# Token-major products of 512 columns, fed by two weight transfers of four row chunks

## The chip, the cores and the metric

The kernel runs on one core of a Trainium2 chip. The metric is the device time of one execution in microseconds (us). The profiler records the span of an execution, every instruction with its start and its length, and the clock that TensorE was granted.

## The reference, cut to what matters

The input is one sequence of 256 positions with 1024 features, and a memory of the same shape. Two blocks of two layers each follow one another. All is float32.

```python
# block 1, twice:
proj = h @ w_in[l]          # 1024 x 5376: xr, gr, q, k, v, g_rnn, g_attn
merged = sigmoid(g_rnn) * (y_rnn @ w_br_rnn) + sigmoid(g_attn) * (y_attn @ w_br_attn)
h = layer_norm(ALPHA * h + merged @ w_out)
h = layer_norm(ALPHA * h + cross_attention(h, mem) @ co_w)   # cq_w, ckv_w inside
h = layer_norm(ALPHA * h + (silu(gate) * up) @ ffn_wo)       # gate, up = h @ ffn_wi
# block 2, twice:
proj = rms_norm(x) @ w_in[l]     # q, k, v, z_a, u_h, z_h, g_a, g_h
merged = sigmoid(g_a) * (y_a @ w_pa) + sigmoid(g_h) * (y_h @ w_ph)
x = x + rms_norm(merged @ w_out)     # y_h: two long convolutions by Fourier transform
```

## The kernel before

Every weight matrix is streamed once. The sync engine's queue brings a chunk of 1 MB (`raw`, three buffers); a chunk is used in two halves of 128 x 1024 numbers. ScalarE rounds each half to a high part `wh` (line 229), VectorE subtracts for the low part `wl` (line 231), and both have four buffers. The activations are kept in such pairs too. One product is three matmuls, high times high, high activation times low weight, low activation times high weight (`mm3`).

There are two forms. `fm` (feature-major) holds the weights still in the array and moves 256 positions past them. `tm` (token-major, lines 406 to 446) holds a 128 x 128 piece of the activations still and moves weight columns past it. It makes the products whose results are wanted with one position per partition: q, k and v of `w_in`, the values of the cross attention (`ckv_w`), `w_out` and `co_w` in block 1, v and z_a of `w_in_2`, and `w_out_2` in block 2. The down projection of the feed-forward (`ff`) has a form of its own, with 512 columns in a matmul.

In `tm`, a group is 256 columns, one chunk of eight row chunks x 256 columns. The first half brings row chunks 0 to 3, the second 4 to 7. In each half the 12 matmuls of the first 128 positions (block 0) come ahead of the 12 of the second (block 1), so a group holds two PSUM tiles, each of which is read out (`evac`) after its last matmul. In the last group block 1's first half is kept back (`hold`), so that block 0 is done early. PSUM has eight banks, four of them in the pool `pa` (`pch`), which `tm` shares with the transposes (`tx`), the attention scores and the Fourier products (`dft`, `c`).

What follows a `tm` depends on the readout. `ln_evac` adds the residual (line 569), takes statistics (571, 574), and normalises (586); then `to_fm` transposes the result (`tx`), applies gain and bias (479 on ScalarE, 485 on VectorE, into `f`) and splits it (`h1h`, `h1l` after the first norm, `h2`, `h3` after the others, 350 and 351), four pairs of row chunks one after another. Then GpSimd multiplies and adds the gain and bias to the token-major copy (605, 606). In block 2 `evo` squares and sums on ScalarE (`jk`, 1679) and multiplies on VectorE (`xo`, 1680), and `evv` makes v and z_a (`za`).

TensorE's and the sync queue's order is written out as the program is generated: a clock `self.t` adds n / 2.4 ns for a matmul of n columns, and stages of the side chains (`pump`) are put in where their estimated times have come. The order on VectorE, ScalarE and GpSimd is set by the tile scheduler.

Of the kernel before, what the change touches and what calls it, by code (L numbers as in the profile page):

```python
# [13 lines left out]
F32 = mybir.dt.float32  # L14
# [6 lines left out]
P = 128  # L21
D = 1024
KD = D // P
S = 256
# [14 lines left out]
LATE = ((0, 0), (1, 0), (1, 1))  # filters whose products fill gaps of the tensor engine  # L39
# [5 lines left out]
# estimated time from the issue of a stage until its results are there, ns  # L45
# [10 lines left out]
def shape_constants():  # L56
# [9 lines left out]
    # odd frequencies of length 2 S: g = f + 1/2 for f < P; those of 2 P - g follow from the  # L66
    # sums over even and odd positions
# [22 lines left out]
class Chunk:  # L90
    """One weight transfer of [P, a, b], used in two halves (by column or by row)."""
# [12 lines left out]
class Net:  # L104
    def __init__(self, ctx, tc, a):
# [12 lines left out]
        # splits of weights wait while a norm holds the vector engine, then queue behind .defer  # L118
# [9 lines left out]
    # ------------------------------------------------------------------ order of issue  # L128
    # Chains are generators that issue a stage and yield the time until the next one can start;
    # the weight stream runs between their stages.  # L130
# [14 lines left out]
    def pump(self):  # L145
        """issues the stages that are due"""
        while True:
            due = [c for c in self.chains if c.ready <= self.t]
            if not due:
                return  # L150
            self.advance(due[0], self.chains)

    def idle(self, until=None):
        """tensor engine has nothing to do: background stage, or let time pass"""
        for c in self.bg:
            if c.ready <= self.t:
                self.advance(c, self.bg)
                return
        nxt = [c.ready for c in self.chains + self.bg if c.ready > self.t]
        if until is not None:  # L160
            nxt.append(until)
        self.t = max(self.t, min(nxt))
# [15 lines left out]
    def run_stream(self, gen):  # L178
        """items: Chunk, or a function to call when its turn comes"""
# [95 lines left out]
    def pin(self):  # L275
        """queues the block's work behind the latest split of weights"""
# [5 lines left out]
    # ------------------------------------------------------------------ tiles  # L282
# [10 lines left out]
    def fmt(self, name, n=2, dt=F32):  # L293
        """feature-major tensor, 4 chunks of [P, S] to a tile"""
# [27 lines left out]
    def tmp(self, shape, name="s", dt=F32):  # L322
        """short-lived: released by the stage that takes it"""
# [3 lines left out]
    def keep(self, shape, name="s", dt=F32):  # L327
        """lives over a few stages of a chain"""
# [19 lines left out]
    # ------------------------------------------------------------------ building blocks  # L348
# [26 lines left out]
    def fm(self, w, c0, ncols, x, evac, kc=KD):  # L375
        """chunks of x() @ w, feature-major; evac(pair, psum)"""
        step = 2048 // kc
        nm = step // 2 // P
        for c in range(c0, c0 + ncols, step):
            box = {}  # L380

            def half(h, wh, wl, c=c, box=box):
                xx = x()
                for i in range(h * nm, h * nm + nm):
# [4 lines left out]
                    # parts of one kind together: the others may still be on their way  # L389
# [16 lines left out]
    def tm(self, w, c0, ncols, x, evac):  # L406
        """chunks of x() @ w, token-major, 256 columns each; evac(chunk, block, psum)"""
        for c in range(c0, c0 + ncols, 256):
            box = {}
            last = c + 256 == c0 + ncols  # L410
            ci = (c - c0) // 256

            def part(h, tb, wt, ps):
                xx = x()
                t = slice(tb * P, tb * P + P)
                if self.start:
                    # the lo part of the weights comes last
                    for j in range(3):
                        for k in range(4):
# [4 lines left out]
                for k in range(4):  # L424
                    g = h * 4 + k
                    self.mm3(ps, self.ch2(xx, g, t), (wt[0][:, k, :], wt[1][:, k, :]),
                             g == 0, g == KD - 1)

            def first(wh, wl, box=box, last=last, part=part):
                box["ps"] = [self.pch([256], "tm") for _ in range(TB)]  # L430
                box["w"] = wh, wl
                part(0, 0, (wh, wl), box["ps"][0])
                if not last:
                    self.pump()
                    part(0, 1, (wh, wl), box["ps"][1])

            def second(wh, wl, box=box, last=last, part=part, ci=ci):
                part(1, 0, (wh, wl), box["ps"][0])
                evac(ci, 0, box["ps"][0])
                self.pump()  # L440
                if last:
                    part(0, 1, box["w"], box["ps"][1])
                part(1, 1, (wh, wl), box["ps"][1])
                evac(ci, 1, box["ps"][1])
            yield Chunk([(None, w[:, c:c + 256].rearrange("(k p) f -> p k f", p=P))], KD, 256,
                        False, [first, second], hold=last)
# [9 lines left out]
    def to_fm(self, src, x, scale=None):  # L456
        """chain: token-major [P, D] per block -> split feature-major x; gain and bias"""
# [31 lines left out]
    def load_x(self, src, name, n=1):  # L489
        """token-major loads, in n column parts"""  # L490
# [7 lines left out]
    # ------------------------------------------------------------------ block 1  # L498
# [58 lines left out]
    def ln_evac(self, t, h, n=256, f=1.0, gb=None, pause=False):  # L557
        """evac for tm: t = f * ALPHA * h + psum, psum being f times the branch, and its
        statistics; normalises a full block, with gain and bias if given"""
# [38 lines left out]
    def ln_co(self, l, i, t, hT):  # L598
        """chain: normalised t -> hT (split feature-major), then t *= gain, t += bias"""
# [8 lines left out]
    def swa_co(self, l, s):  # L608
        """chain: s.q, s.kv token-major -> s.ya feature-major split"""
# [111 lines left out]
    def conv4(self, l, s):  # L721
        """evac: stores the padded pair; a chain convolves it"""
# [23 lines left out]
    def gates(self, l, s):  # L746
        """chunks of the block-diagonal gate products"""
        nc, a = self.nc, self.a

        def half(h, which, wh, wl):  # L750
# [6 lines left out]
            # ig holds tanh(x / 2) = 2 sigmoid(x) - 1  # L757
# [22 lines left out]
    def rnn_co(self, l, s):  # L780
        """chain: gates r, ig and conv output xc -> hidden states times gelu(gr), split"""
# [19 lines left out]
        # the factor 1/2 of the input gate  # L801
# [23 lines left out]
    def merge(self, wa, wb, xa, xb, s, kc, before_b):  # L825
        """s.mg = 2 (sigmoid(a) * (xa @ wa) + sigmoid(b) * (xb @ wb)), feature-major split;
        s.sa, s.sb hold tanh(a / 2), tanh(b / 2) = 2 sigmoid - 1"""
# [26 lines left out]
    def mixer(self, l, s):  # L854
        """s.h, s.hT -> s.t (normalised token-major sums)"""
# [4 lines left out]
        def evq(c, tb, ps):  # L860
# [4 lines left out]
            dst = s.kv[:, tb, :] if c == 4 else s.q[tb][:, c * 256:c * 256 + 256]  # L865
# [55 lines left out]
    def cross_v(self, l, s):  # L921
        def ev(c, tb, ps):
            if c == 0 and tb == 0:
                s.V = [self.hl("cv", [D]) for _ in range(TB)]
            sl = slice(c * 256, c * 256 + 256)
# [3 lines left out]
    def cross_co(self, s, hp):  # L929
        """chain: one head pair of cross attention up to transposed probabilities"""  # L930
# [41 lines left out]
    def cross_out(self, s):  # L972
        """attention-weighted values, feature-major split"""
# [14 lines left out]
    def ffn(self, l, s):  # L988
# [28 lines left out]
        ev_ln = self.ln_evac(lambda: s.t, lambda: s.h, 512,  # L1017
# [49 lines left out]
    def block1(self, s):  # L1067
# [14 lines left out]
        for l in range(DEPTH):  # L1082
            last = l == DEPTH - 1
            # first half of the layer
# [58 lines left out]
    # ------------------------------------------------------------------ block 2  # L1143
    def load_block2(self):
# [16 lines left out]
        # the last layer's columns twice: the halves of its output take the hi and the lo part  # L1161
# [27 lines left out]
    def load_dft(self):  # L1189
        """transforms by parity of the position: [P, parity, cos | -sin], hi and lo"""  # L1190
# [13 lines left out]
    def dft_pair(self, part, src, alloc, name):  # L1204
        """cos (0) or -sin (1) sums of src over even and odd positions"""
# [56 lines left out]
    def filter_piece(self, l, o, res):  # L1262
        """spectrum of the two-sided filter of order o, scaled for the inverse transform"""
# [518 lines left out]
```

## Time and profile before

| | us |
|---|---|
| median of 3 runs | 1610.3 |
| lowest and highest | 1603.89 and 1612.5 |
| span of the profiled execution | 1607.2 |
| TensorE busy | 1530.2 |
| VectorE busy | 1135.2 |
| ScalarE busy | 879.3 |

The page gives the span of the profiled execution, not a time beside it. A busy TensorE means that a matmul was in flight; matmuls overlap, so the rate is read from the distance of two starts, or from a run of matmuls divided by their count.

### The profile page before, as it was taken

How to read it: one execution, taken by the hardware profiler on the slowest of the kernel's cores; microseconds unless marked ns; L12 is line 12 of the kernel's file. 1: busy time of each engine (PE TensorE's matmuls, PEld its weight loads, DVE VectorE, ACT ScalarE, POOL GpSimd, SP SyncE). 2: the span in 40 equal slices, each digit the busy share in tenths (PEclk: the TensorE clock that was granted, in tenths of full speed). 3: DMA queues.
4: the chain of work that ended last, by engine and by line, in shares of the span. 5: the costliest groups of instructions: out<-in, count | busy, mean ns of one | idle time of the engine just before them, and what ended most of it. 6: DMA issues, size and time to landing. Idle time of an engine off the chain costs nothing. (4 is left out here: it accounts for less than half of the span.)

```text
span 1607.2 us, 28221 instructions
## 1 busy us (share of the span) xinstructions
PE 1530.2 (95%) x11740; PEld 1459.3 (91%) x11740; DVE 1135.2 (71%) x1646; ACT 879.3 (55%) x1406; POOL 138.1 (9%) x176
## 2 busy tenths in 40 slices
PE   8999999998999989999989899985999999999997
PEld 7889999998999989899989789975799899898997
DVE  5867677667664587767686776533798978797965
ACT  5789444534444446795446456622645565654753
POOL 5001002002000030010030210000000000000000
PEclk9999999999999999999999999996999999999999
DMA  8444654544555554446555375645454346354452
GB/s 274 132 132 146 223 185 157 172 156 157 165 178 187 186 165 134 130 145 211 196 162 192 105 236 186 202 119 171 131 162 158 123 141 197 132 163 157 133 170 79
DMA packets 228240, 263.10 MB, mean 164 GB/s; under 512 B 6367, under 2 KB 213497, under 8 KB 228112
## 3 DMA queue, kind: packets, MB, share of 16 engines
q1 hardware_dynamic: 221808, 246.43, 47.2%
q0 software_dynamic: 6304, 14.86, 3.8%
q8 instruction: 92, 1.51, 0.4%
q14 instruction: 36, 0.29, 0.1%
HBM read 259.17 MB, written 2.10 MB: 163 GB/s over the span
## 5 line engine op out<-in xcount | busy, mean ns | idle before, releaser
L231 DVE TENSOR_TENSOR wl<-raw,wh 128x1024 fp32r<-128x1024 f32 x464 | 570.1, 1232 | 312.0 <-ACT wh L229 309.2
L229 ACT ACTIVATE wh<-raw 128x1024 fp32r<-128x1024 f32 (+1 forms) x465 | 489.5, 1056 | 477.2 <-PE fm L361 271.3
L361 PE MATMUL fm<-h2h,wh 128*128 128x256 f32 x704 | 174.7, 289 | 25.0 <-ACT wh L229 23.8
L361 PE MATMUL fm<-h2l,wh 128*128 128x256 f32 x704 | 175.1, 290 | 9.9 <-DVE h2l L351 9.9
L361 PE MATMUL fm<-n2h,wh 128*128 128x256 f32 x640 | 176.6, 286 | 1.4 <-ACT n2h L350 1.4
L361 PE MATMUL fm<-n2l,wh 128*128 128x256 f32 x640 | 175.0, 284 | 0.0
L361 PE MATMUL fm<-n2h,wl 128*128 128x256 f32 x640 | 174.5, 283 | 0.0
L361 PE MATMUL fm<-h2h,wl 128*128 128x256 f32 x704 | 173.9, 288 | 0.5 <-DVE wl L231 0.5
L361 PEld LDWEIGHTS fm<-h2h,wh 128*128 128x128 f32 x704 | 126.9, 197 | 29.7 <-ACT wh L229 24.2
L361 PEld LDWEIGHTS fm<-h2l,wh 128*128 128x128 f32 x704 | 126.1, 198 | 11.5 <-DVE h2l L351 11.5
L361 PEld LDWEIGHTS fm<-h2h,wl 128*128 128x128 f32 x704 | 125.7, 197 | 0.8 <-DVE wl L231 0.8
L361 PEld LDWEIGHTS fm<-n2h,wh 128*128 128x128 f32 x640 | 119.9, 192 | 3.5 <-ACT n2h L350 1.9
L361 PEld LDWEIGHTS fm<-n2l,wh 128*128 128x128 f32 x640 | 119.8, 192 | 0.8 <-DVE n2l L351 0.8
L361 PEld LDWEIGHTS fm<-n2h,wl 128*128 128x128 f32 x640 | 119.9, 192 | 0.2
L361 PE MATMUL tm<-wh,mgl 128*128 128x256 f32 x256 | 72.5, 283 | 0.7 <-DVE mgl L351 0.7
L361 PE MATMUL tm<-wh,mgh 128*128 128x256 f32 x256 | 72.4, 283 | 0.0
L361 PE MATMUL tm<-wl,mgh 128*128 128x256 f32 x256 | 72.4, 283 | 0.0
L361 PE MATMUL fm<-h3h,wh 128*128 128x256 f32 x256 | 71.2, 288 | 0.0
L361 PE MATMUL fm<-xTh,wh 128*128 128x256 f32 x256 | 70.9, 287 | 0.0
L361 PE MATMUL fm<-h3l,wh 128*128 128x256 f32 x256 | 70.3, 285 | 0.0
L361 PE MATMUL fm<-h3h,wl 128*128 128x256 f32 x256 | 70.2, 284 | 0.0
L361 PE MATMUL fm<-xTl,wh 128*128 128x256 f32 x256 | 69.8, 283 | 0.0
(440 smaller groups left out, 4185.7 us busy)
## 6 DMA issues: line engine op xcount, KB each, us to landing
raw<-in_w_in_dram SPq DMA_DIRECT2D x89, 1024.0 KB, 5.3
raw<-in_ffn_wi_dram SPq DMA_DIRECT2D x44, 1024.0 KB, 5.1
raw<-in_ffn_wo_dram SPq DMA_DIRECT2D x22, 1024.0 KB, 5.0
raw<-in_w_out_dram SPq DMA_DIRECT2D x16, 1024.0 KB, 5.1
raw<-in_ckv_w_dram SPq DMA_DIRECT2D x16, 1024.0 KB, 5.2
raw<-in_w_br_attn_dram SPq DMA_DIRECT2D x8, 1024.0 KB, 5.1
raw<-in_w_br_rnn_dram SPq DMA_DIRECT2D x8, 1024.0 KB, 5.3
raw<-in_cq_w_dram SPq DMA_DIRECT2D x8, 1024.0 KB, 5.2
```

The source lines that it names most:

```text
L229: hi_ins = self.nc.scalar.activation(hi[:, i:i + q], s[:, i:i + q], AF.Copy)
L231: lo_ins = self.nc.vector.tensor_tensor(lo, s, hi.bitcast(F32), op=ALU.subtract)
L361: self.nc.tensor.matmul(out, lhsT=l, rhs=r, start=start, stop=stop)
```

## The change

A `tm` group is now 512 columns wide, and its weights come as two chunks of four row chunks x 512 columns, so in four halves of two row chunks. In each half six matmuls of 512 columns for block 0 come ahead of six for block 1. The number and size of chunks and halves stay. The 1280 columns of `w_in` make two such groups and one of 256 as before. The readouts take 512 columns at once. Of the last chunk, block 1's first half is still kept back. 2304 matmuls of 256 columns become 1152 of 512; 96 of 256 columns remain in `tm`. The rest of the diff takes comments out.

```diff
@@ -404,46 +404,55 @@
                                lambda wh, wl, f=half: f(1, wh, wl)])
 
     def tm(self, w, c0, ncols, x, evac):
-        """chunks of x() @ w, token-major, 256 columns each; evac(chunk, block, psum)"""
-        for c in range(c0, c0 + ncols, 256):
+
+
+
+        end = c0 + ncols
+        for gi, c in enumerate(range(c0, end, 512)):
+            wd = min(512, end - c)
+            nk = 2048 // wd
             box = {}
-            last = c + 256 == c0 + ncols
-            ci = (c - c0) // 256
-
-            def part(h, tb, wt, ps):
+
+            def part(g, tb, wt, box=box, nk=nk):
                 xx = x()
+                ps = box["ps"][tb]
                 t = slice(tb * P, tb * P + P)
+                n = nk // 2
                 if self.start:
-                    # the lo part of the weights comes last
+
                     for j in range(3):
-                        for k in range(4):
+                        for k in range(n):
                             self.mm(ps, self.ch2(xx, k, t)[j == 1], wt[j == 2][:, k, :],
                                     k == 0 and j == 0, False)
                     self.start = tb == 0
                     return
-                for k in range(4):
-                    g = h * 4 + k
-                    self.mm3(ps, self.ch2(xx, g, t), (wt[0][:, k, :], wt[1][:, k, :]),
-                             g == 0, g == KD - 1)
-
-            def first(wh, wl, box=box, last=last, part=part):
-                box["ps"] = [self.pch([256], "tm") for _ in range(TB)]
-                box["w"] = wh, wl
-                part(0, 0, (wh, wl), box["ps"][0])
-                if not last:
-                    self.pump()
-                    part(0, 1, (wh, wl), box["ps"][1])
-
-            def second(wh, wl, box=box, last=last, part=part, ci=ci):
-                part(1, 0, (wh, wl), box["ps"][0])
-                evac(ci, 0, box["ps"][0])
+                for i in range(n):
+                    k = g * n + i
+                    self.mm3(ps, self.ch2(xx, k, t), (wt[0][:, i, :], wt[1][:, i, :]),
+                             k == 0, k == KD - 1)
+
+            def half(g, hold, wh, wl, box=box, part=part, gi=gi, wd=wd, nk=nk):
+                n_half = 2 * KD // nk
+                if g == 0:
+                    box["ps"] = [self.pch([wd], "tm") for _ in range(TB)]
+                part(g, 0, (wh, wl))
+                if hold and g == n_half - 2:
+                    box["w"] = wh, wl
+                    return
+                if g == n_half - 1:
+                    evac(gi, 0, box["ps"][0])
                 self.pump()
-                if last:
-                    part(0, 1, box["w"], box["ps"][1])
-                part(1, 1, (wh, wl), box["ps"][1])
-                evac(ci, 1, box["ps"][1])
-            yield Chunk([(None, w[:, c:c + 256].rearrange("(k p) f -> p k f", p=P))], KD, 256,
-                        False, [first, second], hold=last)
+                if hold and g == n_half - 1:
+                    part(g - 1, 1, box["w"])
+                part(g, 1, (wh, wl))
+                if g == n_half - 1:
+                    evac(gi, 1, box["ps"][1])
+            for ck in range(KD // nk):
+                hold = c + wd == end and ck == KD // nk - 1
+                src = w[ck * nk * P:(ck + 1) * nk * P, c:c + wd]
+                yield Chunk([(None, src.rearrange("(k p) f -> p k f", p=P))], nk, wd, False,
+                            [lambda wh, wl, f=half, g=2 * ck + h, o=hold: f(g, o, wh, wl)
+                             for h in range(2)], hold=hold)
 
     def rstd(self, out, ss, scale, eps):
         if scale == 1.0:
...
 
-    def ln_evac(self, t, h, n=256, f=1.0, gb=None, pause=False):
-        """evac for tm: t = f * ALPHA * h + psum, psum being f times the branch, and its
-        statistics; normalises a full block, with gain and bias if given"""
+    def ln_evac(self, t, h, n=512, f=1.0, gb=None, pause=False):
+
...
                 s.kv, s.kT = kvt[:, 0], kvt[:, 1]
-            dst = s.kv[:, tb, :] if c == 4 else s.q[tb][:, c * 256:c * 256 + 256]
+            dst = s.kv[:, tb, :] if c == 2 else s.q[tb][:, c * 512:c * 512 + 512]
             nc.scalar.activation(dst, ps, AF.Copy)
...
                 s.V = [self.hl("cv", [D]) for _ in range(TB)]
-            sl = slice(c * 256, c * 256 + 256)
+            sl = slice(c * 512, c * 512 + 512)
             self.split(s.V[tb][0][:, sl], s.V[tb][1][:, sl], ps)
         return self.tm(self.a["ckv_w"][l], 1024, 1024, lambda: self.memT, ev)
...
 
-        ev_ln = self.ln_evac(lambda: s.t, lambda: s.h, 512,
+        ev_ln = self.ln_evac(lambda: s.t, lambda: s.h,
                              gb=(lambda: s.gb) if l == DEPTH - 1 else None,
                              pause=l == DEPTH - 1)
...
                 s.v, s.za = self.slot("v", [TB, 512]), self.slot("za", [TB, 512])
-            sl = slice((c % 2) * 256, (c % 2) * 256 + 256)
-            if c < 2:
-                nc.scalar.activation(s.v[:, tb, sl], ps, AF.Copy)
+            if c == 0:
+                nc.scalar.activation(s.v[:, tb, :], ps, AF.Copy)
             else:
-                z = s.za[:, tb, sl]
+                z = s.za[:, tb, :]
                 nc.scalar.activation(z, ps, AF.Tanh, scale=0.5)
                 nc.vector.scalar_tensor_tensor(z, z, 1.0, ps, op0=ALU.add, op1=ALU.mult)
         yield from self.tm(w, 1024, 1024, x, evv)
...
             nc.gpsimd.dma_start(s.pn, a["post_norm_2"][l:l + 1, :].to_broadcast([P, D]))
-            s.ss = [self.sm.tile([P, 4], F32, tag="pss", name=self.nm("pss")) for _ in range(TB)]
+            s.ss = [self.sm.tile([P, 2], F32, tag="pss", name=self.nm("pss")) for _ in range(TB)]
             s.xo = [self.slot("xo", [D]) for _ in range(TB)]
         yield begin
 
         def evo(c, tb, ps):
-            sl = slice(c * 256, c * 256 + 256)
+            sl = slice(c * 512, c * 512 + 512)
             xo = s.xo[tb]
-            jk = self.tmp([256], "jk2")
+            jk = self.tmp([512], "jk2")
             nc.scalar.activation(jk, ps, AF.Square, accum_out=s.ss[tb][:, c:c + 1])
             nc.vector.tensor_tensor(xo[:, sl], ps, s.pn[:, sl], op=ALU.mult)
-            if c == 3:
+            if c == 1:
                 sm = self.tiny(1, "sm")
                 nc.vector.reduce_sum(sm, s.ss[tb], axis=AX)
                 self.rstd(sm, sm, 1.0 / D, 4e-6)
```

TensorE at the start of `w_in` in layer 1, at the seam between the first and the second half. `tm` is the PSUM tile, `wh` and `wl` are a half of the weights, `h3h` and `h3l` the activations: the tile that is named first holds row chunks 0 to 3, the other 4 to 7. Before:

```order
L361 MATMUL tm_862_6429<-wh_842_6287,h3h_835_6254 128x256
L361 MATMUL tm_862_6429<-wl_843_6288,h3h_835_6254 128x256
L361 MATMUL tm_862_6429<-wh_842_6287,h3l_837_6256 128x256
L361 MATMUL tm_861_6428<-wh_844_6317,h3h_836_6255 128x256
L361 MATMUL tm_861_6428<-wl_845_6318,h3h_836_6255 128x256
L361 MATMUL tm_861_6428<-wh_844_6317,h3l_838_6257 128x256
```

After:

```order
L361 MATMUL tm_846_6001<-wh_826_5859,h3h_819_5826 128x512
L361 MATMUL tm_846_6001<-wl_827_5860,h3h_819_5826 128x512
L361 MATMUL tm_846_6001<-wh_826_5859,h3l_821_5828 128x512
L361 MATMUL tm_845_6000<-wh_828_5889,h3h_819_5826 128x512
L361 MATMUL tm_845_6000<-wl_829_5890,h3h_819_5826 128x512
L361 MATMUL tm_845_6000<-wh_828_5889,h3l_821_5828 128x512
```

Before, the second half of the weights (24 matmuls in) goes with the second tile of activations. After, the second half (12 matmuls in) still works on row chunks 2 and 3, which are in the first tile.

VectorE at the end of `w_out` in layer 0: the last readouts (`t` from `tm`), statistics, norm, and the first gain and bias (`f`). Before:

```order
L586 TENSOR_SCALAR t_353_2679<-t_353_2679,mv_380_2903,rs_381_2905 128x512 x2
L231 TENSOR_TENSOR wl_385_2944<-raw_363_2745,wh_384_2943 128x1024
L569 SCALAR_TENSOR_TENSOR t_354_2680<-x_3_106,tm_379_2876 128x256
L231 TENSOR_TENSOR wl_387_2948<-raw_363_2745,wh_386_2947 128x1024
L571 BN_STATS bst_360_2724<-t_354_2680 128x6
L574 BN_AGGR mv_382_2936<-bst_360_2724 128x2
L450 TENSOR_SCALAR rs_383_2938<-mv_382_2936 128x1
L586 TENSOR_SCALAR t_354_2680<-t_354_2680,mv_382_2936,rs_383_2938 128x512 x2
L231 TENSOR_TENSOR wl_397_2987<-raw_370_2809,wh_396_2986 128x1024
L485 TENSOR_SCALAR f_399_3007<-tx_398_3002,v1_0_546 128x256
```

After:

```order
L595 TENSOR_SCALAR t_349_2575<-t_349_2575,mv_372_2703,rs_373_2705 128x512 x2
L578 SCALAR_TENSOR_TENSOR t_350_2576<-x_3_106,tm_366_2654 128x512
L231 TENSOR_TENSOR wl_377_2732<-raw_357_2611,wh_376_2731 128x1024
L580 BN_STATS bst_361_2636<-t_350_2576 128x6
L231 TENSOR_TENSOR wl_379_2736<-raw_357_2611,wh_378_2735 128x1024
L583 BN_AGGR mv_374_2724<-bst_361_2636 128x2
L459 TENSOR_SCALAR rs_375_2726<-mv_374_2724 128x1
L231 TENSOR_TENSOR wl_389_2775<-raw_364_2651,wh_388_2774 128x1024
L595 TENSOR_SCALAR t_350_2576<-t_350_2576,mv_374_2724,rs_375_2726 128x512 x2
L494 TENSOR_SCALAR f_391_2795<-tx_390_2790,v1_0_442 128x256
```

The wide readout of block 1 comes ahead of both splits of weights (`wl`) instead of between them; a third split has moved ahead of the normalisation of block 1.

## Rows read from the trace of the kernel before

**Rows 1.** The page, part 1: busy time, share and count of each engine.

```profile
span 1607.2 us, 28221 instructions
PE 1530.2 (95%) x11740; PEld 1459.3 (91%) x11740; DVE 1135.2 (71%) x1646; ACT 879.3 (55%) x1406; POOL 138.1 (9%) x176
```

**Rows 2.** Chain of waits, `w_in_2` of layer 0 (start us, us, what, count).

```profile
1224.50 10.08 PE tm L361 x84
1234.58 2.75 PE c L361 x12
```

**Rows 3.** Timeline, TensorE, feed-forward products at full clock (start, us, engine, line, operation).

```profile
401.58 0.40 PE L361 MATMUL ff<-wh,ah 128*128 128x512 f32 x1
...
404.10 0.39 PE L361 MATMUL ff<-wh,al 128*128 128x512 f32 x1
```

**Rows 4.** Waits of TensorE over the span (total us, times, longest).

```profile
PE fm L361 <- DVE h2l L351: 9.9, 7, 2.9
...
PE tm L361 <- DVE h3l L351: 4.4, 4, 1.8
...
PE tm L361 <- DVE mgl L351: 0.7, 1, 0.7
...
PE tx L373 <- DVE f L485: 0.4, 1, 0.4
```

**Rows 5.** Timeline, TensorE, start of `w_in` in layer 1.

```profile
581.88 0.28 PE L361 MATMUL tm<-wl,h3h 128*128 128x256 f32 x1
582.54 0.38 PE L361 MATMUL tm<-wh,h3l 128*128 128x256 f32 x1 [0.39 <-DVE h3l L351]
...
585.32 0.39 PE L361 MATMUL tm<-wh,h3l 128*128 128x256 f32 x1 [1.81 <-DVE h3l L351]
...
590.90 0.58 PE L361 MATMUL tm<-wh,h3l 128*128 128x256 f32 x1 [1.79 <-DVE h3l L351]
591.50 0.41 PE L361 MATMUL tm<-wl,h3h 128*128 128x256 f32 x1
...
593.63 0.41 PE L361 MATMUL tm<-wh,h3l 128*128 128x256 f32 x1
```

**Rows 6.** Stretches of `w_in`, layer 1 (PE, PEld, DVE, ACT, POOL busy, PEclk, DMA).

```profile
581.70:594.10 12.40, 8.01 (x49) 7.20 (x49) 12.02 (x7) 3.52 (x6) 8.78 (x7) 0.86 0.16 46
594.10:617.40 23.30, 23.30 (x196) 23.30 (x196) 12.08 (x27) 11.08 (x16) 0.10 (x1) 1.00 0.65 200
```

**Rows 7.** Timeline, VectorE, same stretch.

```profile
581.40 9.45 DVE L351 TENSOR_TENSOR h3l<-f,h3h 128x512 fp32r<-128x512 f32 x4
590.77 0.68 DVE L351 TENSOR_TENSOR ckl<-fm,ckh 128x512 fp32r<-128x512 f32 x1
591.37 2.35 DVE L231 TENSOR_TENSOR wl<-raw,wh 128x1024 fp32r<-128x1024 f32 x2
```

**Rows 8.** Timeline, GpSimd, same stretch.

```profile
584.68 5.61 POOL L606 TENSOR_TENSOR t<-t,gb 128x1024 f32<-128x1024 f32 x2
```

**Rows 9.** Lines 569 and 571 by form: min/median/max ns.

```profile
L569 DVE SCALAR_TENSOR_TENSOR t<-x,tm x8: 402/414/422, 225.4 to 244.5; 128x256 f32<-128x256 f32 x8
L569 DVE SCALAR_TENSOR_TENSOR t<-t,ff x8: 632/680/687, 565.6 to 1146.2; 128x512 f32<-128x512 f32 x8
L571 DVE BATCH_NORM_STATS2 bst<-t x40: 419/428/686, 225.9 to 1150.1; 128x6 f32<-128x256 f32 x32, 128x6 f32<-128x512 f32 x8
```

**Rows 10.** The page, part 5: weight splits (busy us, mean ns; idle before).

```profile
L231 DVE TENSOR_TENSOR wl<-raw,wh 128x1024 fp32r<-128x1024 f32 x464 | 570.1, 1232 | 312.0 <-ACT wh L229 309.2
```

**Rows 11.** Chain of waits, end of the program.

```profile
1574.78 20.17 PE tm L361 x168
...
1594.97 0.48 ACT jk L1679 x2
...
1595.48 0.42 DVE xo L1680
```

**Rows 12.** Chain of waits, `w_out_2` of layer 0.

```profile
1354.86 0.69 DVE mgl L351
```


## The prediction

> **What bounds the kernel now.** I read the shares of the engines first. TensorE is busy for 1530.2 of the 1607.2 us, VectorE for 71% and ScalarE for 55% [rows 1], so what counts is how fast matmuls follow one another and where TensorE stands still. Second, the chain of waits and the timeline for the rate. 84 `tm` matmuls of 256 columns take 10.08 us, 120 ns each, and 12 Fourier products of 512 columns take 2.75 us right behind them, 229 ns each [rows 2]. The feed-forward's 512-column products, which load a new piece of activations for every matmul as `tm` does, have the first and the twelfth start 2.52 us apart, again 229 ns a step [rows 3]. Two narrow matmuls take 240 ns, one wide one 229. Third, the list of TensorE's waits: the largest of those that touch `tm` or come right behind it are 9.9 us for `h2l`, 4.4 us for `h3l`, 0.7 us for `mgl` [rows 4]. Last, the timeline of the one `tm` that starts before its input is there, `w_in` in layer 1.
>
> **The change part by part.** All is set against the profiled span of 1607.2 us, 3.1 us under the median of 1610.3; the sum is taken off both alike.
>
> *Rate.* There are twelve `tm` of 1024 columns (four in each layer of block 1, two in each layer of block 2), 96 wide matmuls each in place of 192: 23.04 us become 21.98. 1152 wide matmuls x 11 ns = 12.7 us. By the reading of a step from 227.5 to 230 ns it is 11.5 to 14.4. It all counts only where TensorE is the last to be ready, which for the inside of a `tm` it is: apart from the program's start, `w_in` of layer 1 and one `w_out_2`, its matmuls stand step on step.
>
> The Trainium skill, "TensorE: Matmul & The Clock Gate", section "Back-to-back issue gap", gives the distance of two isolated matmuls at full clock as N / 2.4 ns plus about 2.5 ns. By that rule a wide matmul saves 2.5 ns, an estimate of 2.9 us for 1152. The rows disagree: 120 ns is 13 above 256 / 2.4 = 107, and 229 is 16 above 213, with a load of the array ahead of each matmul. The measured steps decide.
>
> *`w_in` of layer 1.* It begins while the third norm of layer 0 is still being split. Four `h3l` pairs come off VectorE in 9.45 us [rows 7], some 2.8 us apart, because GpSimd's `t` runs at the same time (two in 5.61 us) [rows 8]; the `h3l` starts of TensorE are at 582.54, 585.32, about 588.1 and 590.90 [rows 5]. Before, the first half of the weights needs two pairs and the second the two others, and there is work only for 0.7 us after each odd pair. Then TensorE's clock falls: from 590.90 the matmuls start (593.63 - 591.50) / 10 = 213 ns apart, the level of 1.2 GHz, after waits of 1.81 and 1.79 us [rows 5], and the stretch has a mean granted clock of 0.86 [rows 6]. The whole `w_in` lasts from 581.7 to 617.4, 35.7 us, for 240 x 0.120 = 28.8 us of work: 6.9 us are lost. After, each half of two row chunks needs exactly one pair and holds 12 x 0.229 = 2.75 us of work, as much as a pair takes to come. TensorE waits 0.5 us for the first and goes on to 590.6. The fourth half then needs its low weights, and this `wl` stands on VectorE behind the fourth `h3l` and `ckl`, where two of them ran from 591.37 in 2.35 us [rows 7]: the first is there at 592.5. A wait of about 1.8 us stays. From 592.4 there are 60 wide matmuls, 13.7 us, and the 48 narrow ones of the last group, 5.8: the end is at 611.9 in place of 617.4. Of these 5.5 us 1.1 are in the rate already, 4.4 are new. Bounds: nothing, if VectorE's order is worse than I read it, and 6.9 if the wait for `wl` goes as well.
>
> *`w_out_2` of layer 0.* Row chunks 6 and 7 came in the second half after 24 matmuls, and `mgl` ended at 1355.55 [rows 12]; TensorE stood for 0.7 [rows 4]. Now they come in the fourth half, 36 wide matmuls (8.2 us) into the stage. The wait goes, 0.8 us with its step; nothing is late in its place, since the low weights of each half are split every 2.75 us at 1.23 each [rows 10].
>
> *Tails.* The last readout is wider. A residual takes 0.68 in place of 0.41 us, the statistics likewise 0.68 at most in place of 0.43 [rows 9]. Behind the last matmul of block 1 these two are in the chain to the transposes, so 0.5 us comes on at each of four `ln_evac` ends (`w_out` and `co` in two layers): 2.0 us. In `w_out` of layer 0 VectorE's order also carries three splits of 1.23 us [rows 10] between the readout of block 1 and the first `f`, as before, so I put nothing there. At each `w_out_2` it is ScalarE's `jk` (0.48 for two operations [rows 11], some 0.2 more at the wider form by the ratio of the residual) and `xo` (0.42, 0.27 more by the same), 0.5 x 2 = 1.0 us. The PSUM tiles: a group holds two of the four banks of `pa` for four halves (11 us) and not two (5.8), so the transposes of probabilities in the cross attention and those at the head of the program change places among two banks. The nearest row is a transpose's wait of 0.4 us for `f` [rows 4]; I take 0.2 at each of two cross attentions and 0.4 for the first `w_in`: 0.8 in all. Together 3.8 us. Bounds: none, where VectorE is ahead of TensorE's end; one split more (1.23) and 0.5 at each of eight places, 14 us.
>
> *At nothing.* The number of transfers and their bytes stay; a pair of halves now asks for 1 MB in 5.5 us in place of 5.8, and the stretch of `w_in` that runs at the full rate moved 200 GB/s with the DMA engines at 0.65 [rows 6], so cover is left. If it were not there, 12 stages x 4 transfers x 0.3 us would give the rate back. The number of operations on VectorE and ScalarE falls. The long standstill in the second feed-forward and its transfers are not touched.
>
> Sum: -12.7 - 4.4 - 0.8 + 3.8 = -14.1 us, a span of 1593 and a median of 1596. With the bounds: from -14.4 - 6.9 - 0.8 = -22 to -11.5 + 14 = +2.5.
>
> **The rivals.**
>
> *The tails eat it.* The rate is won inside a stage, but the next stage starts when a chain on VectorE ends, and this chain has wider operations and as many splits. For it: TensorE already waits 9.9 us in seven places for `h2l`, behind the norms [rows 4]. Against: the chain begins at the last matmul, which comes 1.06 us earlier, and the order of splits in it is nearly the same. If a split falls in at each of the eight ends, the gain is 17.9 less 8 x (0.5 + 0.8): about -7.5 us, 1603.
>
> *No rate in `tm`.* The step of a matmul may go with its columns alone, so that a wide one takes 240 ns where the activations are the held side. For it: at 1.2 GHz a narrow step is 213 ns [rows 5], just 256 / 1.2, with nothing fixed in it. Against: the wide steps of 229 ns of two other products [rows 2, 3], one of which holds activations in the same way. Without the 12.7 the sum is -1.4 us: 1609. The rule of the Trainium skill lies between: with its 2.9 the sum would be -4.3.
>
> *Slower: the banks.* The two tiles of a group hold half of `pa` all through a stage, so a norm's four `tx` tiles share the two other banks: the third and the fourth wait until VectorE has read the first and the second. Where GpSimd's `t` runs at that time, one such read takes a pair's 2.8 us, and after such waits the clock falls, at 16 narrow steps x 93 ns = 1.5 us a time [rows 5]. Two waits and one fall are 7.1 us at a norm; at four norms 28 us against 17.9 won, +10 us: 1621. It decides from three norms on. For it: the waits for `h2l` of up to 2.9 us [rows 4]. Against: GpSimd's multiplication is issued only behind the last `tx`, and today transposes wait for `f` once in the whole run, 0.4 us [rows 4].
>
> That the change doesn't do what it says can be left out: the order on TensorE has 1152 matmuls of 512 columns in the places of the 2304.
>
> **How the numbers follow.** The sum as worked out, 0.60 (likely -10 to -19); the tails, 0.22; no rate, 0.05; the banks, 0.07; more than the sum (no tails, no wait for `wl`), 0.06, around 1590. A time within 0.5%, 8 us, can't be told from no change; the runs of before themselves lie 0.5% apart. Faster by more than that: nearly all of the first (0.57), the last, and half of the tails, 0.74. Within: the other half, no rate, a little of the banks, 0.19. Slower: 0.07. The predicted time is 1596 us. The range leaves out 0.1 on each side: 1585, the best sum with the median, less a run's scatter, to 1607, where the tails end.
>
> **What would show it.** In the profile after: 96 wide `tm` matmuls in 22.0 us where no wait falls in, 229 ns a step (at 240 there was no rate to win). At `w_in` of layer 1 waits of 0.5 us for `h3l` and about 1.8 for a `wl`, a granted clock of 1.00 behind it, and 30 us from its start to its end. No wait for `mgl`. In the list of waits, `h1l` and `h2l` up by some 2 us in all and hardly a wait of `tx`; if these two grow by 6 or more, the tails were right, and if `tx` waits for `f` in each norm, the banks. The prediction is wrong if the steps are right and the span is still above 1602.

## The result: 1590.5 us, 1.1% faster

The changed kernel takes 1590.49 us in the median (1588.39 to 1590.96), the kernel before 1611.39 beside it; the ratio is 0.9888 (0.9860 to 0.9915). A second measurement gave 0.9877 (0.9855 to 0.9899). The forecast was 1596 with a range of 1585 to 1607.

The page after, part 1, and the largest waits of TensorE that bear on the change (us in total, times, longest), which answer to [rows 1] and [rows 4]:

```profile
span 1588.3 us, 25810 instructions
PE 1515.2 (95%) x10588; PEld 1394.7 (88%) x10588; DVE 1124.5 (71%) x1594; ACT 876.3 (55%) x1366; POOL 140.1 (9%) x176
```

```profile
PE fm L361 <- DVE h2l L351: 10.2, 7, 2.9
...
PE fm L361 <- DVE wl L231: 3.4, 2, 2.9
PE tx L373 <- DVE t L595: 2.6, 2, 2.3
...
PE fm L361 <- DVE h1l L351: 1.8, 1, 1.8
PE tm L361 <- DVE wl L231: 1.8, 1, 1.8
```

Three more waits changed. Before:

```profile
PE fm L361 <- DVE h1l L351: 3.6, 2, 1.8
PE dft L361 <- DVE dsc L1446: 3.5, 2, 1.7
...
PE fd L361 <- ACT fr L1345: 1.9, 1, 1.9
```

After, `h1l` as above, `dsc` in `dft` gone, and:

```profile
PE fd L361 <- ACT fr L1354: 2.6, 1, 2.6
```

The span is 18.9 us shorter, TensorE's busy time 15.0. `h3l` and `mgl` are off the list; `wl` in `tm` and `t` in `tx` are new or larger; `h2l` is where it was.

The rate, in the chain of waits of `w_in_2`, layer 0 (start, us, what, count), beside [rows 2]:

```profile
1209.83 9.55 PE tm L361 x42
1219.38 2.72 PE c L361 x12
```

42 wide matmuls are 227 ns each. A stage of 96 lasts 21.79 us and not 23.04.

`w_in` of layer 1, the timeline of TensorE, beside [rows 5]:

```profile
579.93 0.40 PE L361 MATMUL tm<-wl,h3h 128*128 128x512 f32 x1
580.47 0.50 PE L361 MATMUL tm<-wh,h3l 128*128 128x512 f32 x1
...
588.49 0.39 PE L361 MATMUL tm<-wh,h3h 128*128 128x512 f32 x1
590.63 0.50 PE L361 MATMUL tm<-wl,h3h 128*128 128x512 f32 x1 [1.75 <-DVE wl L231]
590.97 0.40 PE L361 MATMUL tm<-wh,h3l 128*128 128x512 f32 x1
```

and its stretches (PE, PEld, DVE, ACT, POOL busy, granted clock, DMA share, GB/s):

```profile
579.70:590.20 10.50, 9.03 (x39) 6.53 (x37) 10.50 (x6) 5.20 (x7) 8.77 (x7) 1.00 0.12 45
590.20:609.90 19.70, 19.27 (x108) 16.95 (x109) 13.38 (x29) 8.93 (x11) 0.10 (x1) 1.00 0.75 234
```

Ahead of 580.47 TensorE stands for some 0.3 us; between 580.47 and 588.49 there is no wait; one of 1.75 us for a `wl` stays, the granted clock stays at 1.00, and the stage lasts 30.2 us in place of 35.6.

Where the time went, from the starts of TensorE's stages in both traces (negative: won). `cov`, further down, is the product of the cross attention with its values; `fd` and `fh` make the filters of block 2's long convolutions, `ds` its attention scores; `rb` is a transpose in block 1's attention.

| place | us |
|---|---|
| `w_in`, layer 1 | -5.4 |
| `w_out_2`, layer 0 (rate 1.25, `mgl` 0.9) | -2.2 |
| the other `tm` stages | -11.0 |
| `fm` behind `w_out` of layer 1 (waits for `h1l`) | -3.1 |
| `dft` behind v and z_a, two layers | -3.3 |
| `ff` of layer 1, its long standstill | -0.9 |
| `fm` behind it (mean granted clock 0.86, before 0.79), and `rb` (1.00, before 0.50) | -1.5 |
| `tx` behind `w_out` of layer 0 | +1.9 |
| `fd` behind `w_out_2` of layer 0 | +1.9 |
| `ds` behind the `dft`, two layers | +2.0 |
| `tx` behind `w_out` of layer 1 | +0.8 |
| all else, to the end of TensorE's work | +1.1 |
| sum | -19.7 |

From the last matmul to the end of the span it is 0.7 us longer, with wider `jk` and `xo`.

### The profile page after: what moved, and what is told of

Its sections match the earlier page's. It is cut to its first block, busy times and chain, and to the rows that moved or that the text cites. A ratio compares the mean times of both kernels' runs of the same rounds, so it can differ in the third digit from the quotient of the medians.

```text
span 1588.3 us, 25810 instructions
## 1 busy us (share of the span) xinstructions
PE 1515.2 (95%) x10588; PEld 1394.7 (88%) x10588; DVE 1124.5 (71%) x1594; ACT 876.3 (55%) x1366; POOL 140.1 (9%) x176
## 5 line engine op out<-in xcount | busy, mean ns | idle before, releaser
L361 PE MATMUL fm<-xTh,wl 128*128 128x256 f32 x256 | 69.8, 283 | 0.0
L361 PE MATMUL ff<-wh,ah 128*128 128x512 f32 x176 | 69.1, 392 | 0.0
L361 PE MATMUL ff<-wl,ah 128*128 128x512 f32 x176 | 68.7, 390 | 0.0
```

Of the source, the lines that this page charges most:

```text
L361: self.nc.tensor.matmul(out, lhsT=l, rhs=r, start=start, stop=stop)
```

## The experiments

### Narrow matmuls in the changed kernel

```diff
-                    self.mm3(ps, self.ch2(xx, k, t), (wt[0][:, i, :], wt[1][:, i, :]),
-                             k == 0, k == KD - 1)
+                    for o in range(0, wd, 256):
+                        self.mm3(ps[:, o:o + 256], self.ch2(xx, k, t),
+                                 (wt[0][:, i, o:o + 256], wt[1][:, i, o:o + 256]),
+                                 k == 0 and o == 0, k == KD - 1 and o == wd - 256)
```

(likewise in the branch for the program's first stage)

> The changed kernel with every 512-column tm matmul made as two of 256 columns; transfers, halves, PSUM tiles and wide readouts stay. Theory A (rate first): 1152 matmuls give back two steps of 120 ns less one of 227, 13 ns each, 14 to 15 us, so some 1604 us against 1590 for the changed kernel and 0.4% below the kernel before; the wait for mgl stays away and w_in of layer 1 still ends about 4 us earlier than before. Rival B (the gain lies in waits that fell away with the order of row chunks and readouts): within 5 us of the changed kernel.

1603.88 us, ratio 0.9972 (0.9959 to 0.9985), against 0.9877 of the changed kernel measured beside it: 15 us. Its chain of waits has the steps of 120 ns again, in the same halves and with the same readouts:

```profile
1219.54 10.08 PE tm L361 x84
1229.62 2.75 PE c L361 x12
1232.37 11.53 PE tm L361 x96
```

`w_in` of layer 1 is 4.5 us shorter than before, without any wider matmul. Theory A holds, rival B falls.

### Narrow readouts in the changed kernel

```diff
-                    evac(gi, 0, box["ps"][0])
+                    for o in range(0, wd, 256):
+                        evac(2 * gi + o // 256, 0, box["ps"][0][:, o:o + 256])
```

(likewise for block 1, with the readouts of before)

> The changed kernel with its wide matmuls, each 512-column PSUM tile read out in two operations of 256 columns. Theory A: the tm stages stay at 227 ns a step; the rest moves only as VectorE's order and the tails do, within 4 us of the changed kernel. The stop in the dft behind v and z_a of w_in_2 (2.1 us in each layer before, 0.45 now) stays away if the row-chunk order brought that, and comes back (some 1.7 us a layer) if the single wide z_a readout did. Rival C (wide readouts cost at the tails): 3 us faster than the changed kernel.

1595.66 us, ratio 0.9918 (0.9898 to 0.9937): 7 us slower than the changed kernel measured beside it. That is against both: more than A allowed, and the other sign than C. The stages themselves stay at 227 ns a step. By place, against the first profile of the changed kernel, it loses in the `dft` behind v and z_a (1.3 in each layer, of which 1.0 comes back in `ds`), in `cov` and the `fm` behind `co` of layer 1 (0.7 and 1.2), in `fd` (1.6), 2 us at the long standstill in the feed-forward of layer 1 and behind it, and 1.2 behind the last matmul; 1.4 of it comes back in an `fm` and an `fh` of that layer's feed-forward. So narrow readouts, both of a tile at once, are no cheaper at the tails.

### The row-chunk order alone

Both edits together: transfers and halves of the changed kernel, matmuls and readouts of 256 columns.

> Only the order of row chunks is changed: two transfers of four row chunks by 512 columns, matmuls and readouts of 256 columns. Theory A: w_in of layer 1 about 4.4 us shorter than before, the wait for mgl gone (0.8), tails up to 3 us either way: about 1605, 5 us under the kernel before. Rival B: close to the changed kernel, 1590 to 1595.

1606.46 us, ratio 0.9988 (0.9975 to 1.0000): hardly faster than before, and less than the 5 us of theory A; rival B falls. `w_in` of layer 1 is 4.5 us shorter and the `fm` behind `w_out` of layer 1 4.6, but `tx` in `w_out` of layer 0 takes 3.2 longer, the `fm` behind `co` 1.4, `fd` 4.2 and the stretch behind the last matmul 1.8. In this form of the kernel the waits that the order takes away are spent again, most of them at the tails.

The four ratios split the change. The order of row chunks alone gives 0.12%. Wide matmuls give another 0.70% behind narrow readouts (0.9988 to 0.9918) and 0.95% behind wide ones (0.9972 to 0.9877), 11 and 15 us. Wide readouts give 0.16% with narrow matmuls and 0.41% with wide ones, 3 and 7 us. The parts don't simply add up, but the difference of 4 us is no larger than the scatter of these ratios.

### The changed kernel again

> The changed kernel itself beside the three others: 0.989 of the kernel before, 1590 us.

1588.6 us, as expected. Its profile is 3.3 us shorter than the first one, 1.6 of it in the `fm` behind `w_out` of layer 0, 0.8 in the first `w_in` and 1.2 in `fd` in block 2: the same wait of 2.6 us ahead, and then a mean granted clock of 0.69 in one profile and 1.00 in the other (columns as above; the first row is of the first profile, the second of the other):

```profile
1361.60:1365.70 4.10, 4.04 (x12) 3.13 (x13) 3.40 (x6) 3.05 (x7) 0.81 (x9) 0.69 0.00 0
```

```profile
1359.70:1362.70 3.00, 2.81 (x12) 2.32 (x13) 2.30 (x5) 3.00 (x7) 0.81 (x9) 1.00 0.00 0
```

A step behind a wait that differs by 1 to 2 us between two kernels may therefore be no effect of the edit. Of the 1.9 us of `fd` in the table, 0.7 is the longer wait for `fr`; the other 1.2 is not there in this second profile.

### w_in of block 1 as before

```diff
-        yield from self.tm(w, 2048, 1280, x, evq)
+        yield from self.tm_narrow(w, 2048, 1280, x, evq)
```

(`tm_narrow` is `tm` of the kernel before, with its readout of q)

> The changed kernel, but w_in of block 1 (both layers) in groups of 256 columns over all row chunks as before. Theory A: w_in of layer 1 loses 4.4 us of waits and half clock again and 1.2 of rate, that of layer 0 about 0.8 of rate: 6.5 us over the changed kernel, 1595. Rival D (the wait for h3l is only passed on to the next stage, since VectorE is what is late): under 2.5 us over it.

1598.38 us, ratio 0.9937 (0.9917 to 0.9957), 8 to 10 us over the changed kernel (0.9888 and 0.9877), where theory A said 6.5. 5.3 us come at this one stage in layer 1, and `h3l` is back in the list of waits with the 4.4 us of before:

```profile
PE tm L361 <- DVE h3l L351: 4.4, 4, 1.8
```

Rival D falls: what is won here is not handed on. In layer 0 the stage is 1.6 us longer than in the first profile; the other 1 to 3 us lie at places behind a wait, and which of them the edit causes is not shown.

### The norm ahead of the splits

The loss at `tx` in `w_out` of layer 0 has a reading in the trace after. VectorE there (start, us, line, operation), and GpSimd's power of the norm, after and before:

```profile
246.01 0.15 DVE L459 TENSOR_SCALAR rs<-mv 128x1 f32<-128x1 f32 x1
246.09 1.22 DVE L231 TENSOR_TENSOR wl<-raw,wh 128x1024 fp32r<-128x1024 f32 x1
247.76 1.00 DVE L595 TENSOR_SCALAR t<-t,mv,rs 128x512 f32<-128x512 f32 x2 [0.45 <-POOL rs L463]
```

```profile
246.25 1.48 POOL L463 TENSOR_TENSOR rs<-rs,mhalf 128x1 f32<-128x1 f32 x1 [4.88 <-DVE rs L459]
```

```profile
247.00 0.55 POOL L454 TENSOR_TENSOR rs<-rs,mhalf 128x1 f32<-128x1 f32 x1 [4.55 <-DVE rs L450]
```

The third split, moved ahead of the normalisation by the scheduler, runs beside a power of one number per partition, which then takes 1.48 us in place of 0.55; the split takes its 1.22 us as ever. The edit takes the splits out of there:

```diff
+                        n_ins = nc.vector.tensor_scalar(x[:, s], x[:, s], mv[:, 0:1], rs,
+                                                        op0=ALU.subtract, op1=ALU.mult)
+                if gb is None and not pause and tb == TB - 1:
+                    self.defer = n_ins      # the normalisation of block 1
```

> The changed kernel with the weight splits that stand inside the norm of block 1's readout (w_out of both layers, first norm) queued behind that norm on VectorE. If the wait of the first tx for t (2.3 us in w_out of layer 0, from the splits and from GpSimd's power beside one of them) costs by itself, 2 us or more are won. If the chain to h1l decides, the tx wait goes and the wait for h1l behind it grows by as much: within 1 us of the changed kernel.

1590.44 us, ratio 0.9888 (0.9871 to 0.9904): no gain. The power is back at its old length:

```profile
243.43 0.55 POOL L463 TENSOR_TENSOR rs<-rs,mhalf 128x1 f32<-128x1 f32 x1 [2.88 <-DVE rs L459]
```

`tx` starts without a wait and is 2.5 us shorter, and the `fm` behind it is 2.2 longer. I had named `h1l` for that, and it stays at 1.8 us; the list of waits names the splits that now come later, with 4.4 us for one `wl` where it was 2.9:

```profile
PE fm L361 <- DVE wl L231: 5.5, 3, 4.4
```

### GpSimd's gain and bias after the split

```diff
+        tok = self.tiny(1, "tok")
+        go = nc.gpsimd.tensor_copy(tok, hT[1][1][:, 3, S - 1:S].bitcast(F32))
+        with self.tc.issue_after(go.ins):
             for tb in range(TB):
                 nc.gpsimd.tensor_tensor(t[tb], t[tb], gb[0], op=ALU.mult)
                 nc.gpsimd.tensor_tensor(t[tb], t[tb], gb[1], op=ALU.add)
```

> The changed kernel with GpSimd's gain and bias of each norm (t times gb, t plus gb) started only after the last low half of the split (a one-column copy of it comes ahead on GpSimd). My claim: these operations beside the split make each h-l take 2.2 to 2.9 us instead of 0.7. Then the four h-l of a norm come in some 3 us and most of TensorE's waits for h1l, h2l and h3l (12 us in the list) and half-clock stretches behind them go: 8 to 14 us under the changed kernel. If the pace of h-l has another cause, no change.

1571.65 us, ratio 0.9776 (0.9761 to 0.9790), 2.2% under the kernel before and 16 to 18 us under the changed kernel, more than the 8 to 14 that I claimed. The four `h3l` in the timeline of VectorE, in the changed kernel and then in this one:

```profile
579.33 9.51 DVE L351 TENSOR_TENSOR h3l<-f,h3h 128x512 fp32r<-128x512 f32 x4
```

```profile
567.88 2.48 DVE L351 TENSOR_TENSOR h3l<-f,h3h 128x512 fp32r<-128x512 f32 x4
570.28 0.68 DVE L351 TENSOR_TENSOR ckl<-fm,ckh 128x512 fp32r<-128x512 f32 x1
570.88 6.51 DVE L231 TENSOR_TENSOR wl<-raw,wh 128x1024 fp32r<-128x1024 f32 x2
```

2.48 us where it was 9.51 (9.45 before [rows 7]). GpSimd's work now lies beside the weight splits, 3.2 to 3.4 us each in place of 1.2:

```profile
570.57 5.74 POOL L617 TENSOR_TENSOR t<-t,gb 128x1024 f32<-128x1024 f32 x2
576.27 6.72 POOL L618 TENSOR_TENSOR t<-t,gb 128x1024 f32<-128x1024 f32 x2
```

With four buffers TensorE does not wait for the splits there: `w_in` of layer 1 lasts 27.6 us without a gap. All waits for `h1l`, `h2l` and `h3l` are off its list. The Trainium skill, "SBUF — State Buffer", section "Who interferes with whom", says that a VectorE instruction with two inputs from SBUF contends with a GpSimd one that reads SBUF, and calls the ports that they share an exclusive lock; the two `h3l` rows agree, 9.51 us against 2.48.

### The same edit in the kernel before

> The kernel before with the same edit of GpSimd's gain and bias. With the waits for h3l gone by that, w_in of layer 1 has nothing left to win from the order of row chunks: some 12 to 18 us under the kernel before, and the difference to the same edit in the changed kernel is rate and tails alone, about 14 us in place of 19. If the h-l keep their pace, no change.

1585.53 us, ratio 0.9861 (0.9846 to 0.9876). The edit is worth 22 us here, more than the 12 to 18 expected, and 16 to 18 in the changed kernel; the change is worth 14 with it (0.9861 less 0.9776), as expected, and 18 to 20 without. 4 us of that difference are the waits for `h3l` in `w_in` of layer 1, which edit and change both take away: with the edit in both, that stage differs by 1.5 us in the two traces, the rate of its 96 wide matmuls and little more. Elsewhere the two pairs of traces differ by up to 5 us a place, in both directions, which is not explained here.

### Both edits, and the queue on GpSimd

> The changed kernel with both edits: GpSimd's gain and bias after the last low half, and the weight splits behind the first norm. With the wait for h1l behind it gone, the 2.3 us wait of the first tx in w_out of layer 0 now decides there and goes: 2 us under the late gain alone, about 1569. If splits that come later are missed by TensorE, no gain.

1572.45 us, ratio 0.9787 (0.9769 to 0.9806), not distinguishable from the late gain alone; the 1569 expected did not come. `tx` in `w_out` of layer 0 is 2.5 us shorter and 1.8 of it are still there behind the next stages; at the end they are gone, in steps of 0.5 to 1.6 us behind waits. What they are was not settled.

> As the run before, but the second norm of layer 1 keeps its gain and bias where they were. There the late gain holds up the filter weights' transfers on GpSimd's queue (fwr is issued some 15 us later against the norm, and TensorE waits 5.2 us for fwo). If that queue is what costs: the 4 to 6 us lost there come back, but the 8.5 us won in the h2l waits of that norm go too, so 2 to 4 us slower than the run before. If the queue costs nothing: 8 us slower.

1571.57 us, ratio 0.9779 (0.9761 to 0.9797), within the scatter of the run before: the 2 to 4 us of the first case did not come, nor the 8 of the second. At the place it goes as the first case said: the `fm` behind that norm is 8.8 us longer, the `ff` and `fm` after it 6.4 shorter. The wait for `fwo`, 5.4 us in the run before, is down to 1.0:

```profile
PE fh L361 <- ACT fwo L1295: 5.4, 1, 5.4
```

```profile
PE fh L361 <- ACT fwo L1297: 1.0, 1, 1.0
```

In sum nothing clear of the scatter. Of the 8.8 us that a late gain wins in this norm, 4.4 are lost at `fwo`, whose transfers stand behind it on GpSimd's queue; the other 2 us lost in `ff` and `fm` are not shown to be the queue's.

### Narrow z_a alone

```diff
-                nc.scalar.activation(z, ps, AF.Tanh, scale=0.5)
-                nc.vector.scalar_tensor_tensor(z, z, 1.0, ps, op0=ALU.add, op1=ALU.mult)
+                    z = s.za[:, tb, o]
+                    nc.scalar.activation(z, ps[:, o], AF.Tanh, scale=0.5)
+                    nc.vector.scalar_tensor_tensor(z, z, 1.0, ps[:, o], op0=ALU.add, op1=ALU.mult)
```

(for the two halves `o` of a tile; v likewise)

> The changed kernel with v and z_a of w_in_2 alone read out in two operations of 256 columns. If the single readout moved the first score (dsc) ahead of a weight split on VectorE, the stop in the dft behind them comes back (some 1.3 us a layer) and the later one in ds (1.0) goes: within 1 us of the changed kernel in all, and the readouts of the norms then carry the rest of the 7 us that narrow readouts cost everywhere. If the narrow readouts cost by their number, 2 us slower.

1591.18 us, ratio 0.9905 (0.9890 to 0.9920), 3 to 5 us over the changed kernel (0.9888 and 0.9877) and 1.8 over it in the first profile. Within 1 us was expected, so the total does not rule out the second case; the place does speak for the first. VectorE behind v and z_a, first in the changed kernel, then in this one:

```profile
1235.35 0.68 DVE L1647 SCALAR_TENSOR_TENSOR za<-za,tm 128x512 f32<-128x512 f32 x1
1235.95 0.68 DVE L1455 SCALAR_TENSOR_TENSOR dsc<-ds,bias 128x512 f32<-128x512 f32 x1
1236.55 1.93 DVE L231 TENSOR_TENSOR wl<-raw,wh 128x1024 fp32r<-128x1024 f32 x1
```

```profile
1237.01 0.41 DVE L1648 SCALAR_TENSOR_TENSOR za<-za,tm 128x256 f32<-128x256 f32 x1
1237.34 1.21 DVE L231 TENSOR_TENSOR wl<-raw,wh 128x1024 fp32r<-128x1024 f32 x1
1238.48 0.41 DVE L1648 SCALAR_TENSOR_TENSOR za<-za,tm 128x256 f32<-128x256 f32 x1
1238.81 1.27 DVE L1455 SCALAR_TENSOR_TENSOR dsc<-ds,bias 128x512 f32<-128x512 f32 x2
```

and TensorE's `dft` in this one:

```profile
1239.03 0.47 PE L361 MATMUL dft<-zh,dft 128*128 128x512 f32 x1 [1.47 <-DVE za L1648]
```

With two readouts a split comes between them and the `dft` waits for the tile that the second frees. The `dft` is 1.3 us longer in each layer, `ds` 1.0 shorter, as expected. So the single readout won that place, by what stands between two readouts and not by its own length. What carries the rest of the 7 us of narrow readouts everywhere stays open.

## Why the prediction was right, point by point

*The bound.* Right: TensorE's rate. The step sizes were a little off. A wide step in `tm` is 227 ns, not 229, and the `tm` stages without their waits won 13.5 us, not 12.7; with matmuls made narrow again 15 us are lost. This term is the largest part of the gain. By the rule of the Trainium skill, "TensorE: Matmul & The Clock Gate", section "Back-to-back issue gap", which is for isolated matmuls, it would have been 2.9 us, an estimate. In this stream, with a load of the array ahead of each matmul, the measured 15 us decide.

*`w_in` of layer 1.* Right, in size and in nearly each row: some 0.3 us ahead of the first `h3l` (0.5 forecast), no wait between pairs, 1.75 us for the `wl` (1.8), the granted clock at 1.00, 5.4 us shorter (5.5). Its reason, a pair of low halves every 2.8 us because GpSimd works beside them, is shown by the late gain: 2.48 us for all four.

*`mgl`.* Right: 0.9 us beside the rate (0.8).

*Tails.* The term that failed, and with it most of the miss of 4.8 us in the span. I put it at +3.8, from the length of the readouts and the banks. Outside `tm`, stage by stage, the traces show 8.6 us lost and 9.6 won, and 0.7 lost behind the last matmul: -0.3 in all, and 2.3 us less still in the second profile. The list of waits went the other way too: `h1l` and `h2l` together came down from 13.5 to 12.0 us where I had put them up by 2, and `tx` now waits 2.6 us for `t` where I saw hardly a wait.

The step was to price the wider readout alone and to take VectorE's order for the same: "as before, so I put nothing there". In `w_out` of layer 0 it was not as before. Between the readout of block 1 and its normalisation the order before has one split of weights and the order after three, and with the slower power that made 1.9 us at `tx`. This error hid part of the larger one. The order of VectorE behind `w_out` of layer 1 and behind z_a took waits away (3.1 and 3.3 us, of which 2.0 are lost again in `ds`) that I had not looked at, and 2.4 us were won at the long standstill and where TensorE's clock was low, which I had put at nothing. That the total still lay within the range is in part luck: losses and gains that I had not foreseen in place or in size nearly cancel. Whether the 1.9 us at `tx` cost anything by the end is not shown, since taking them away gained nothing.

*Rivals.* The tails did not eat the gain, the rate was there in `tm`, and the banks did not decide, though they show: with narrow readouts the `dft` waits 1.5 us for the tile that z_a frees, and `tx` waits 1.2 us for `f` where it was 0.4 [rows 4]. The price of the tails' rival was too low by its own figures: a split is 1.23 us [rows 10] and not the 0.8 in its sum, which would have left a gain of 4 us and not 7.5.

*At nothing.* Right for the transfers: 234 GB/s in the full-rate part of `w_in`, against 200 [rows 6]. ScalarE has one new wait for `raw`, 2.0 us at a `ckv_w`, but no `tm` stage as a whole is longer than before.

## What to carry to other kernels

Where matmuls of a stage stand step on step, count steps from two shapes in the same trace: two steps of 120 ns became one of 227, and the 13 ns of difference, 1152 times, made 15 us of 1607 here. Where an input comes in pieces, let one piece of weights need one piece of it; whether the rest of the kernel keeps what that wins has to be measured, as the row-chunk order alone gave hardly anything in sum. And the readout's neighbours on its engine have to be read from the new order before the readout's own length is worth an estimate.

## What the runs showed of the hardware

VectorE's subtraction with both inputs in SBUF and GpSimd's element-wise work hold each other up: a low half took 0.68 us alone and 2.88 beside GpSimd's multiplications and additions (three of the four `h3l` in the changed kernel, 9.51 us in all), a weight split 1.2 alone and up to 3.4 beside it. GpSimd's instruction of 128 x 1024 took 2.85 us beside these low halves and 3.38 beside splits. That fits two engines that take turns by whole instructions, since the two differ by 0.53 us as a split and a low half do. Where the split came first, it kept its 1.22 us and the GpSimd power of one number a partition took 1.48 in place of 0.55 (1.47 to 1.48 at all three such places in the changed kernel). Moving GpSimd's work out of the chain, without making any of it less, took 16 to 18 us from the changed kernel, nearly as much as the change itself won.
